# A hybrid decoder layer on one core: the bias table's DMAs on ScalarE's queue, other buffers for the gates, and an output projection that starts in two passes

## The chip, the core and the metric

The kernel runs on one core of a Trainium2 chip. The core has a matrix engine (TensorE, PE in the profile; its weight loads are PEld), VectorE (DVE), ScalarE (ACT), GpSimd (POOL) and SyncE (SP), which here issues DMAs. Each engine works through its own list of instructions in order, and semaphores hold an instruction until what it reads is there. The metric is the device time of one execution in microseconds.

## What is computed

One layer of a decoder, 512 tokens of width 1024, batch 1, float32:

```python
h = rms_norm(x, norm_mix)
qa, ka, va, qg, kg, vg, glr, rg = split(h @ w_in)
o_a = moba_attention(qa, ka, va, rp_table)           # 8 heads of 64, blocks of 256, relative bias
log_a = log_sigmoid(glr @ w_gate_up + b_gate) / 16
o_g = gla_chunked(qg, kg, vg, log_a)                  # 4 heads, decayed linear attention
o_g = rms_norm(o_g, g_norm) * silu(rg)
x = x + concat([o_a, o_g]) @ w_out
x = x + cross_attention(rms_norm(x, norm_xattn), rms_norm(mem, norm_mem))   # 256 memory tokens, 4 heads
x = x + square(relu(rms_norm(x, norm_mlp) @ w_up)) @ w_down
return rms_norm(x, norm_final)
```

With 512 tokens and blocks of 256 every past block is chosen, so the block-sparse group is plain causal attention with a bias by distance.

## The kernel before, in words

Activations lie transposed: 8 tiles of 128 rows (k-tiles) by 512 tokens. Each float32 operand is split into a high and a low float16 half, and a product is three float16 products (high by high, high by low, low by high: L231 to L233, for token-major results L246 to L248, in the later matrix products L1183 to L1185). A weight tile of 128x1024 float32 is loaded by SP into a buffer `wst` (5 of them, L114); ScalarE makes the high half `whl` (10 buffers, L115) and VectorE the low half (L116). `Weights.order` lists the tiles in the order in which they are loaded, and `get` asks for some tiles ahead.

TensorE's order is written by hand, that of the other engines is made by a scheduler from the program. Work that nobody waits for soon is a generator in a queue, `Fill`: `fill(n)` lets TensorE do n steps of it, and a step of a 128x512 product is one k-tile, three products. So the gated linear attention (class `Gla`, two passes for two pairs of heads) is laced with `vg` (values), `qk` (queries and keys of the attention), `xk` and `xv` (keys and values of the memory tokens) at L744 to L786. In `Gla`, a decay chain `e`, `g`, `b` gives scaled queries and keys (`qF`, `kF`, `qz`, `kz`, `z`), which TensorE multiplies into `psL`, `ps64`, later `st` and `go`; `gss` is the norm's sum. Then come the attention pairs 0 to 3 (class `Pair`, L787 and following): scores `s` at L809, `trans`, and `attn_out` one pair later, laced with `va`, `qk2`, `qk3` and the gates `rg`.

`rg_steps(h)` (L527) computes x times sigmoid of x by exponentials: after the product `rg` VectorE evicts it to `x`, ScalarE and VectorE work in turns in `e` and `u`, then the result multiplies `mixf[4 + h]` and is split into `mix[4 + h]`. The three float32 tiles came from one ring of 3 buffers (`yx`, shared with `qkf`, the eviction of `qk`). `early_steps` (L865) starts the output projection of row tiles 0 to 3 on the six k-tiles of `mix` that don't depend on the last two pairs (0, 1 from attention, 4 to 7 from the gates); `residual_steps` adds k-tiles 2 and 3 later.

The relative bias is made once: a small product (`bv`), a copy `bvec` by VectorE, a DMA to DRAM `bscr1` (L723) and a second DMA (L726) that spreads it over 128 rows, each shifted by one, into `bscr` (1.5 MB). `load_bias` reads from there (L739). The second DMA reads what the first wrote, so the queue that issues it waits for the first to land.

Of the kernel before, what the change touches and what calls it, by code (L numbers as in the profile page):

```python
# [10 lines left out]
F32 = mybir.dt.float32  # L11
# [5 lines left out]
P = 128  # L17
T = 512
# [21 lines left out]
def hybrid_block_kernel(  # L40
# [3 lines left out]
    nc = tc.nc  # L44
# [10 lines left out]
    pst = ctx.enter_context(tc.tile_pool(name="pst", bufs=2))  # L55
# [3 lines left out]
    def bank(tag, bufs, name):  # L59
        return psum.tile([P, 512], F32, tag=tag, bufs=bufs, name=name)  # L60

    def gbank(name):
        return bank("pg", 3, name)

    def sbank(name):
        return bank("ps", 5, name)
# [139 lines left out]
    W.add(("tt", 8), w_tt[8])  # L206
    for n in range(4):
        W.add(("va", n), w_vv[n])
    for n in (2, 6, 3, 7, 9, 10, 11):
        W.add(("tt", n), w_tt[n])  # L210
    for nm, ap in (("out", w_out), ("xq", w_xq), ("xo", w_xo)):
        for n in range(8):
# [12 lines left out]
    def gemm_steps(ps, key, act, c0=0, c1=T, kts=range(8), start=True, stop=True, base=0, look=LOOK, **kw):  # L225
        wt = W.get(key, look).rearrange("p s (k c) -> p s k c", k=8)
        kts = list(kts)
        for i, kt in enumerate(kts):
            a = act[base + kt]
            st, sp = start and i == 0, stop and i == len(kts) - 1  # L230
            PE.matmul(ps, wt[:, 0, kt, :], a[:, 0, c0:c1], start=st, stop=False, **kw)  # L231
            PE.matmul(ps, wt[:, 0, kt, :], a[:, 1, c0:c1], start=False, stop=False, **kw)  # L232
            PE.matmul(ps, wt[:, 1, kt, :], a[:, 0, c0:c1], start=False, stop=sp, **kw)  # L233
            yield
# [5 lines left out]
    def gemm_tok_steps(ps, keys, act, t0, look=LOOK):  # L240
        ws = [W.get(k, look).rearrange("p s (k c) -> p s k c", k=2) for k in keys]
        for kt in range(8):
            w = ws[kt // 2]
            a = act[kt]
            st, sp = kt == 0, kt == 7
            PE.matmul(ps, a[:, 0, t0:t0 + P], w[:, 0, kt % 2, :], start=st, stop=False)  # L246
            PE.matmul(ps, a[:, 0, t0:t0 + P], w[:, 1, kt % 2, :], start=False, stop=False)
            PE.matmul(ps, a[:, 1, t0:t0 + P], w[:, 0, kt % 2, :], start=False, stop=sp)  # L248
            yield
# [24 lines left out]
    fill = Fill()  # L274

    def split(dst_h, dst_l, src, scale):
        ACT.activation(dst_h, src, AF.Copy, scale=scale)  # L277
        DVE.scalar_tensor_tensor(dst_l, src, scale, dst_h, op0=ALU.mult, op1=ALU.subtract)  # L278
# [76 lines left out]
    mix = [m.bitcast(F16).rearrange("p (s t) -> p s t", s=2) for m in mixf]  # L355
# [15 lines left out]
    def tmp(nm):  # L371
        return p1.tile([P, T], F32, tag="yx", bufs=3, name=nm)
# [12 lines left out]
    for j in range(4):  # L385
        for i, _ in enumerate(W.pieces(2)):
# [5 lines left out]
            sq = acc if k % 4 == 0 else pst.tile([P, 512], F32, tag="sq", bufs=2, name=f"sqx{k}")  # L392
# [6 lines left out]
    for j in range(4):  # L399
        w = W.tiles["gqk", j][1].rearrange("p s (k n c) -> p s k n c", k=2, n=4)  # L400
        for i in range(2):
            x = act0[2 * j + i]
            for n, ps in enumerate(gps):
                for a, b in ((0, 0), (0, 1), (1, 0)):
                    PE.matmul(ps, w[:, a, i, n, :], x[:, b, :], start=(j == 0 and i == 0 and a == 0 and b == 0),
                              stop=(j == 3 and i == 1 and a == 1), skip_group_check=True)
# [7 lines left out]
    def evict(dst, ps, scale):  # L414
        DVE.scalar_tensor_tensor(dst, ps, scale * IX, wx, op0=ALU.mult, op1=ALU.mult)

    for n, ps in enumerate(gps):
        t = (gq, gk)[n % 2][n // 2] = pg.tile([P, T], F32, name=f"gqk{n}")
# [9 lines left out]
    for i in range(2):  # L428
        for a, b in ((0, 0), (0, 1), (1, 0)):
            for j in range(4):  # L430
                kt = 2 * j + i
                PE.matmul(psg[32 * j:32 * j + 32, :], wg[:, a, kt, :], act0[kt][:, b, :],
                          start=(i == 0 and a == 0 and b == 0), stop=(i == 1 and a == 1),
# [12 lines left out]
    def va_steps(t):  # L446
        ps = gbank(f"va{t}")
        yield from gemm_tok_steps(ps, [("va", j) for j in range(4)], act0, t * P)
        va[t] = p1.tile([P, 2, 512], F16, tag="va", bufs=4, name=f"vas{t}")
        split(va[t][:, 0, :], va[t][:, 1, :], ps, wxt[:, t:t + 1])  # L450
# [3 lines left out]
    def qk_steps(p):  # L454
        for lst, col, sc in ((aq, 0, 0.125), (ak, 4, 1.0)):
            ps = gbank(f"qk{col + p}")
            yield from gemm_steps(ps, ("tt", col + p), act0)
            nm = f"qks{col + p}"
            lst[p] = p1.tile([P, 2, T], F16, tag="qk", bufs=6, name=nm) if p < 3 else pt.tile([P, 2, T], F16, name=nm)
            y = tmp(f"qkf{col + p}")  # L460
            evict(y, ps, SA * sc)
            split(lst[p][:, 0, :], lst[p][:, 1, :], y, 1.0)
# [64 lines left out]
    def rg_steps(h):  # L527
        ps = gbank(f"rg{h}")
        yield from gemm_steps(ps, ("tt", 8 + h), act0)
        x, e, u = (tmp(f"rg{c}{h}") for c in "xeu")  # L530
        evict(x, ps, 1.0)
        ACT.activation(e, x, AF.Exp, scale=-1.0)
        DVE.tensor_scalar(e, e, 1e30, None, op0=ALU.min)
        ACT.activation(u, e, AF.Ln, bias=one_c)
        ACT.activation(u, u, AF.Exp, scale=-1.0)

        DVE.scalar_tensor_tensor(e, e, 1.0, u, op0=ALU.add, op1=ALU.mult)
        DVE.scalar_tensor_tensor(u, e, 2.0, u, op0=ALU.subtract, op1=ALU.mult)
        DVE.scalar_tensor_tensor(x, x, -1.0, u, op0=ALU.mult, op1=ALU.mult)
        DVE.tensor_tensor(x, x, mixf[4 + h], op=ALU.mult)  # L540
        split(mix[4 + h][:, 0, :], mix[4 + h][:, 1, :], x, 1.0)


    class Gla:
# [175 lines left out]
    bvec = pst.tile([P, 512], F32, tag="sq", bufs=2, name="bvec")[0:8, :NDIST]  # L720
    DVE.tensor_copy(bvec, psb[0:8, 0:NDIST])
    bscr1 = pdr.tile([8, NDIST], F32, name="bscr1")
    nc.sync.dma_start(bscr1, bvec)  # L723
    bscr = pdr.tile([8, P, T], F32, name="bscr")

    nc.sync.dma_start(  # L726
        bass.AP(tensor=bscr.tensor, offset=bscr.offset, ap=[[P * T, 8], [T + 1, P], [1, NDIST]]),
        bass.AP(tensor=bscr1.tensor, offset=bscr1.offset, ap=[[NDIST, 8], [0, P], [1, NDIST]]),
    )
# [4 lines left out]
    def load_bias(p):  # L734
        bias[p] = []
        for hh in range(2):
            h = 2 * p + hh
            bq = (pt if p % 2 else p1).tile([P, T], F32, tag="bq", bufs=2, name=f"bq{h}")
            nc.sync.dma_start(bq[:, 256:], bscr[h, :, 127:383])  # L739
            POOL.tensor_copy(bq[:, :256], bq[:, 256:257].to_broadcast([P, 256]))  # L740
            bias[p].append(bq)
# [3 lines left out]
    fill.add(*[xv_steps(c, t) for c in range(2) for t in range(2)])  # L745
    gl = []
    for pr in range(2):
        fill(5)
        gl.append(Gla(pr))
        if pr == 0:  # L750
            pw_ = sbank("wxt")
            for t in range(4):
                PE.transpose(pw_[:, t * P:t * P + P], wx[:, t * P:t * P + P], ident)
            DVE.tensor_scalar(wxt, pw_.rearrange("p (n t) -> p n t", t=P)[:, :, 0], SA * IX, None, op0=ALU.mult)
    for pr in range(2):
        if pr == 1:
            load_bias(0)
        G = gl[pr]
        a = G.prep_fine()
        fill(18 if pr == 0 else 6)  # L760
        G.banks()
        G.small(0, a)
        for i, s in enumerate((8, 16)):
            a = G.prep_level(s)
            fill(4)
            G.small(128 + 128 * i, a)
        a = G.prep_level(32)
        fill(6)
        G.mid(a[0])
        a = G.prep_level(64)  # L770
        fill(6)
        G.large(a[0])
        G.prep_cross()
        fill(6)
        G.keys()
        fill(6)
        G.states()
        fill(6)
        G.outp()
        fill(6)  # L780
        for hh in range(2):
            G.norm(hh)
            fill(4)
        if pr == 0:
            fill.add(rg_steps(0))
# [76 lines left out]
    NPRE = 4  # L862
    early = {}

    def early_steps():  # L865
        for n in range(NPRE):
            early[n] = sbank(f"out{n}")
            yield from gemm_steps(early[n], ("out", n), mix, 0, T, (0, 1, 4, 5, 6, 7), stop=False, skip_group_check=True)

    def residual_steps(nm, act, hf, ssq):  # L870
        c0 = hf * HT
# [17 lines left out]

    HT = T // 2  # L890
    ssq = sums("out", *HALVES)
    fill.add(*[va_steps(t) for t in range(4)], qk_steps(2), qk_steps(3), *[rg_steps(h) for h in (1, 2, 3)])
    pairs = {}
    for i in range(5):
        if i < 4:
            pairs[i] = Pair(i)
            if i < 3:
                load_bias(i + 1)
        if i in (2, 3):
            fill.until({2: 4, 3: 3}[i])  # L900
        if i == 4:
            fill.drain()
            load_xr()
            fill.add(early_steps(), residual_steps("out", mix, 0, ssq[0]))
        for g in range(4):
            if i < 4:
                pairs[i].score(3 - g)
                fill(5 if i < 3 else 3)
            elif g > 0:
                fill(4)  # L910
            if 1 <= i < 4 and g == 3:
                fill.until(5)
                attn_out(pairs.pop(i - 1))
        if i < 4:
            pairs[i].trans()
            fill(4)
# [333 lines left out]
    for j in range(2):  # L1250
        for m in range(4):
            u = Unit(m, j)
# [31 lines left out]
    u, v = Unit(2, 1), Unit(3, 1)  # L1284
# [127 lines left out]
```

## Time and profile before

| what | us |
|---|---|
| runs of the kernel before | 723.3, 726.82, 727.47; median 726.82 |
| the profiled execution | 728.34 |
| its span, from first to last record | 726.6 |
| TensorE busy | 685.3 (94%) |
| VectorE busy | 553.3 (76%) |
| ScalarE busy | 416.6 (57%) |
| GpSimd busy | 75.1 (10%) |
| mean granted clock of TensorE | 0.976 |

The granted clock is 1.00 when TensorE has its full 2.4 GHz and 0.50 at 1.2 GHz. The times of all rows are microseconds from the start of the span; a row's bracket says how long the engine was idle before it and what ended that.

### The profile page before, as it was taken

The numbers are of one execution on the slowest core, as the hardware profiler recorded it, in microseconds if no ns is written. First come the engines' busy times: TensorE is split into PE (matmuls) and PEld (weight loads), VectorE is DVE, ScalarE is ACT, GpSimd is POOL, SyncE is SP. The second block draws the span as 40 slices with busy tenths as digits, with TensorE's granted clock in tenths as the row PEclk, the third lists the DMA queues.
The fourth block names the chain that finished last, engine by engine and source line by source line (L and its number), as shares of the span: only waits on it lengthen the run. The fifth ranks groups of instructions, "written<-read, shape, count | busy, mean of one in ns | idle before, by whom it ended". The sixth has DMA issues, their size and how long they took to land.

```text
span 726.6 us, 13422 instructions
## 1 busy us (share of the span) xinstructions
PE 685.3 (94%) x5352; PEld 469.6 (65%) x5352; DVE 553.3 (76%) x987; ACT 416.6 (57%) x800; POOL 75.1 (10%) x90
## 2 busy tenths in 40 slices
PE   8998959999899499799999999999999999999995
PEld 3444637444444168588888864458888866478884
DVE  6978378868968615847647899989887889999725
ACT  7655366677757315546535676555444666665533
POOL 4050000000000024200013200000000000003211
PEclk9999979999999799999999999999999999999998
DMA  8871009742837503306411513113333342314003
GB/s 301 268 254 41 1 6 295 262 135 80 240 89 214 160 1 106 127 3 174 145 30 47 188 53 122 58 59 117 117 116 117 116 143 90 117 34 143 29 1 117
DMA packets 57059, 85.68 MB, mean 118 GB/s; under 512 B 32123, under 2 KB 37540, under 8 KB 56996
## 3 DMA queue, kind: packets, MB, share of 16 engines
q1 hardware_dynamic: 56996, 84.82, 37.3%
q8 instruction: 42, 0.69, 0.4%
q14 instruction: 21, 0.17, 0.1%
HBM read 75.36 MB, written 3.68 MB: 109 GB/s over the span
## 4 chain that ended last, share of the span: by engine, by line
PE 59%; DVE 8%; ACT 3%; issue 1%; POOL 1%; DVEq 0%; ACTq 0%; POOLq 0%
PE up L232 6%; PE up L231 6%; PE up L233 6%; PE a L1183 4%; PE a L1185 4%; PE a L1184 4%; PE xq L232 2%; PE xq L233 2%; PE xq L231 2%; PE c L1184 2%; PE c L1183 2%; PE c L1185 2%; DVE whl L116 2%; PE out L232 1%; PE out L233 1%
## 5 line engine op out<-in xcount | busy, mean ns | idle before, releaser
L116 DVE SCALAR_TENSOR_TENSOR whl<-wst,whl 128x1024 f16<-128x1024 f32 (+1 forms) x165 | 195.2, 1190 | 26.7 <-ACT whl L115 26.1
L115 ACT ACTIVATE whl<-wst 128x1024 f16<-128x1024 f32 (+1 forms) x165 | 165.4, 1013 | 38.4 <-PE a L1185 7.9
L231 PEld LDWEIGHTS <-whl 128*128 128x128 f16 x744 | 73.6, 99 | 48.0 <-ACT whl L115 7.9
L232 PEld LDWEIGHTS <-whl 128*128 128x128 f16 x744 | 73.6, 99 | 47.7 <-issue 13.5
L233 PEld LDWEIGHTS <-whl 128*128 128x128 f16 x744 | 73.6, 99 | 46.3 <-issue 6.9
L231 PE MATMUL up<-act,whl 128*128 128x512 f16 (+1 forms) x224 | 78.1, 349 | 0.0
L233 PE MATMUL up<-act,whl 128*128 128x512 f16 (+1 forms) x224 | 78.1, 349 | 0.0
L232 PE MATMUL up<-act,whl 128*128 128x512 f16 (+1 forms) x224 | 78.1, 349 | 0.0
L1183 PE MATMUL a<-t,whl 128*128 128x256 f16 x192 | 52.3, 273 | 1.1 <-ACT v L1200 1.1
L1184 PE MATMUL a<-t,whl 128*128 128x256 f16 x192 | 52.3, 273 | 0.0
L1185 PE MATMUL a<-t,whl 128*128 128x256 f16 x192 | 52.3, 273 | 0.0
L1184 PEld LDWEIGHTS <-whl 128*128 128x128 f16 x456 | 44.6, 98 | 6.9 <-issue 1.5
L1183 PEld LDWEIGHTS <-whl 128*128 128x128 f16 x456 | 44.6, 98 | 5.2
L1185 PEld LDWEIGHTS <-whl 128*128 128x128 f16 x456 | 44.6, 98 | 5.0
L231 PE MATMUL out<-mix,whl 128*128 128x256 f16 (+1 forms) x104 | 31.6, 304 | 8.3 <-ACT mix L277 8.3
L232 PE MATMUL xq<-act,whl 128*128 128x256 f16 x128 | 35.5, 277 | 3.3 <-DVE act L278 3.3
L231 PE MATMUL xq<-act,whl 128*128 128x256 f16 x128 | 35.5, 277 | 0.9 <-ACT act L277 0.9
L233 PE MATMUL xq<-act,whl 128*128 128x256 f16 x128 | 35.5, 277 | 0.0
L233 PE MATMUL xo<-ox,whl 128*128 128x256 f16 x128 | 34.9, 273 | 0.0
L231 PE MATMUL xo<-ox,whl 128*128 128x256 f16 x128 | 34.9, 273 | 0.0
L232 PE MATMUL xo<-ox,whl 128*128 128x256 f16 x128 | 34.9, 273 | 0.0
L277 ACT ACTIVATE t<-hs 128x512 f16<-128x512 f32 x32 | 19.8, 624 | 24.0 <-DVE hs L1065 23.8
(334 smaller groups left out, 1646.7 us busy)
## 6 DMA issues: line engine op xcount, KB each, us to landing
wst<-in_w_up SPq DMA_DIRECT2D x32, 512.0 KB, 3.5
wst<-in_w_down SPq DMA_DIRECT2D x32, 512.0 KB, 3.8
wst<-in_w_tt SPq DMA_DIRECT2D x12, 512.0 KB, 4.7
wst<-in_w_vv SPq DMA_DIRECT2D x8, 512.0 KB, 5.1
wst<-in_w_xk SPq DMA_DIRECT2D x8, 512.0 KB, 11.2
wst<-in_w_xv SPq DMA_DIRECT2D x8, 512.0 KB, 5.0
wst<-in_w_out SPq DMA_DIRECT2D x8, 512.0 KB, 3.8
wst<-in_w_xq SPq DMA_DIRECT2D x8, 512.0 KB, 3.5
```

What stands on the lines that cost most here:

```text
L115: ACT.activation(wt[:, 0, c], stg[:, c], AF.Copy, scale=SW)
L116: DVE.scalar_tensor_tensor(wt[:, 1, c], stg[:, c], SW, wt[:, 0, c], op0=ALU.mult, op1=ALU.subtract)
L231: PE.matmul(ps, wt[:, 0, kt, :], a[:, 0, c0:c1], start=st, stop=False, **kw)
L232: PE.matmul(ps, wt[:, 0, kt, :], a[:, 1, c0:c1], start=False, stop=False, **kw)
L233: PE.matmul(ps, wt[:, 1, kt, :], a[:, 0, c0:c1], start=False, stop=sp, **kw)
L277: ACT.activation(dst_h, src, AF.Copy, scale=scale)
L1183: PE.matmul(ps, w[:, 0, kt, :], b[:, 0, c], start=st, stop=False, skip_group_check=not start)
L1184: PE.matmul(ps, w[:, 0, kt, :], b[:, 1, c], start=False, stop=False, skip_group_check=not start)
L1185: PE.matmul(ps, w[:, 1, kt, :], b[:, 0, c], start=False, stop=sp, skip_group_check=not start)
```

## The change

Five edits; the functions' arithmetic is the same.

```diff
-    for n in (2, 6, 3, 7, 9, 10, 11):
+    for n in (2, 6, 9, 3, 7, 10, 11):
         W.add(("tt", n), w_tt[n])
...
         yield from gemm_steps(ps, ("tt", 8 + h), act0)
-        x, e, u = (tmp(f"rg{c}{h}") for c in "xeu")
+        x = tmp(f"rgx{h}")
+        e, u = (pst.tile([P, 512], F32, tag=t, bufs=2, name=f"rg{t}{h}") for t in ("sq", "nw"))
...
-    nc.sync.dma_start(bscr1, bvec)
+    nc.scalar.dma_start(bscr1, bvec)
...
-    nc.sync.dma_start(
+    nc.scalar.dma_start(
         bass.AP(tensor=bscr.tensor, offset=bscr.offset, ap=[[P * T, 8], [T + 1, P], [1, NDIST]]),
...
-        fill(5)
+        fill(8 if pr == 0 else 4)
         gl.append(Gla(pr))
...
-        fill(18 if pr == 0 else 6)
+        fill(20 if pr == 0 else 6)
...
-        for n in range(NPRE):
-            early[n] = sbank(f"out{n}")
-            yield from gemm_steps(early[n], ("out", n), mix, 0, T, (0, 1, 4, 5, 6, 7), stop=False, skip_group_check=True)
+        for kts in ((0, 1, 4, 5), (6, 7)):
+            for n in range(NPRE):
+                if n not in early:
+                    early[n] = sbank(f"out{n}")
+                yield from gemm_steps(early[n], ("out", n), mix, 0, T, kts, start=kts[0] == 0, stop=False, skip_group_check=True)
...
-    fill.add(*[va_steps(t) for t in range(4)], qk_steps(2), qk_steps(3), *[rg_steps(h) for h in (1, 2, 3)])
+    fill.add(*[va_steps(t) for t in range(4)], qk_steps(2), rg_steps(1), qk_steps(3), rg_steps(2), rg_steps(3))
...
-            fill.until({2: 4, 3: 3}[i])
+            fill.until({2: 4, 3: 2}[i])
```

From L527 on a line of the changed kernel has a number higher by 1, from `early_steps` on by 2 or 3. In the rows below a name ends in its tile's number and a running number of the allocation.

ScalarE, early: `whl13` is the last weight split before the memory tokens are split (`mix0` to `mix3`; `accm`, `sqm` are their squares), `e0` opens the decay chain of the first head pair, `vgs` evict `vg`. Before:

```order
L115 ACTIVATE whl13_444<-wst13_443 128x1024
L483 ACTIVATE mix0_105<-memf0_841,gmem_400 128x256 x2
L486 ACTIVATE accm_845<-memf0_841 128x512
L483 ACTIVATE mix1_106<-memf1_842,gmem_400 128x256 x2
L490 ACTIVATE sqm1_860<-memf1_842 128x512
L483 ACTIVATE mix2_107<-memf2_843,gmem_400 128x256 x2
L490 ACTIVATE sqm2_867<-memf2_843 128x512
L483 ACTIVATE mix3_108<-memf3_844,gmem_400 128x256 x2
L490 ACTIVATE sqm3_874<-memf3_844 128x512
L115 ACTIVATE whl14_879<-wst14_878 128x1024
L556 ACTIVATE e0_467<-z0_463,gsb_76 128x512
```

The same place in the changed kernel:

```order
L115 ACTIVATE whl13_444<-wst13_443 128x1024
L724 DMA bscr1_413<-bvec_411 8x384
L483 ACTIVATE mix0_105<-memf0_803,gmem_400 128x256 x2
L486 ACTIVATE accm_807<-memf0_803 128x512
L483 ACTIVATE mix1_106<-memf1_804,gmem_400 128x256
L727 DMA bscr_415<-bscr1_413 8x128x384
L557 ACTIVATE e0_476<-z0_472,gsb_76 128x512
L444 ACTIVATE vgs0_491<-vg0_417,wxt_125 128x512
L558 ACTIVATE e0_476<-e0_476 128x512
L444 ACTIVATE vgs1_539<-vg1_493,wxt_125 128x512
L559 ACTIVATE e0_476<-e0_476,ones_78 128x512
L444 ACTIVATE vgs2_566<-vg2_541,wxt_125 128x512
```

The two DMAs stand between the first steps on the memory tokens, `e0` and three `vgs` have moved ahead of the rest of these steps, and `whl14` has moved behind them.

ScalarE, the weight splits `whl16` to `whl20` (the tiles 3 to 7 of `xk`). Before, behind steps of the second head pair (`kF_1`, `qz8_1`, `qz16_1`):

```order
L577 ACTIVATE kF_1_1166<-dF_1_1163 128x512
L594 ACTIVATE qz8_1_1253<-d8_1_1251 128x32x8
L595 ACTIVATE kz8_1_1254<-d8_1_1251 128x32x8
L594 ACTIVATE qz16_1_1329<-d16_1_1327 128x16x16
L115 ACTIVATE whl16_976<-wst16_975 128x1024
L115 ACTIVATE whl17_981<-wst17_980 128x1024
L115 ACTIVATE whl18_986<-wst18_985 128x1024
L115 ACTIVATE whl19_991<-wst19_990 128x1024
L115 ACTIVATE whl20_1045<-wst20_1044 128x1024
```

In the changed kernel, among steps of the first head pair (`qz16_0`, `z32_0`, `z64_0`):

```order
L595 ACTIVATE qz16_0_686<-d16_0_684 128x16x16
L596 ACTIVATE kz16_0_687<-d16_0_684 128x16x16
L115 ACTIVATE whl14_841<-wst14_840 128x1024
L657 ACTIVATE et0_890<-b0_481 128x4
L115 ACTIVATE whl15_914<-wst15_913 128x1024
L115 ACTIVATE whl16_976<-wst16_975 128x1024
L595 ACTIVATE z32_0_740<-d32_0_738 128x8x32
L596 ACTIVATE z32_0_740<-d32_0_738 128x8x32
L595 ACTIVATE z64_0_787<-d64_0_785 128x4x64
L596 ACTIVATE z64_0_787<-d64_0_785 128x4x64
L115 ACTIVATE whl17_981<-wst17_980 128x1024
L115 ACTIVATE whl18_986<-wst18_985 128x1024
```

The splits of one head pair's time have moved into the other's.

VectorE, ahead of the scores of attention pair 3: `qkf7` and `qks7` evict and split its keys, `rgx1` is gate 1, `pq2` the split probabilities of pair 2, `mix1` the output of pair 1. Before:

```order
L415 SCALAR_TENSOR_TENSOR qkf7_2334<-qk7_2263,wx_124 128x512
L814 TENSOR_SCALAR sm4_2_2170<-sm4_2_2170 128x2
L116 SCALAR_TENSOR_TENSOR whl47_2752<-wst47_2751,whl47_2752 128x1024
L278 SCALAR_TENSOR_TENSOR qks7_2333<-qkf7_2334,qks7_2333 128x512
L820 RECIPROCAL sm4_2_2170<-sm4_2_2170 128x4
L821 TENSOR_SCALAR sm4_2_2170<-sm4_2_2170 128x4
L838 SCALAR_TENSOR_TENSOR pq2_0_2238<-p2_1_0_2286,sm4_2_2170,pq2_0_2238 128x2x128
L838 SCALAR_TENSOR_TENSOR pq2_1_2239<-p2_1_1_2288,sm4_2_2170,pq2_1_2239 128x2x128
L838 SCALAR_TENSOR_TENSOR pq2_0_2238<-p2_0_0_2316,sm4_2_2170,pq2_0_2238 128x128
L838 SCALAR_TENSOR_TENSOR pq2_1_2239<-p2_0_1_2318,sm4_2_2170,pq2_1_2239 128x128
L278 SCALAR_TENSOR_TENSOR mix1_106<-o1_2359,mix1_106 128x512
L415 SCALAR_TENSOR_TENSOR rgx1_2399<-rg1_2338,wx_124 128x512
```

In the changed kernel (the other steps of gate 1 stand ahead of these rows):

```order
L278 SCALAR_TENSOR_TENSOR mix5_110<-rgx1_2258,mix5_110 128x512
L822 TENSOR_SCALAR sm4_2_2170<-sm4_2_2170 128x4
L278 SCALAR_TENSOR_TENSOR qks3_2342<-qkf3_2343,qks3_2342 128x512
L278 SCALAR_TENSOR_TENSOR mix1_106<-o1_2368,mix1_106 128x512
L839 SCALAR_TENSOR_TENSOR pq2_0_2238<-p2_1_0_2295,sm4_2_2170,pq2_0_2238 128x2x128
L839 SCALAR_TENSOR_TENSOR pq2_1_2239<-p2_1_1_2297,sm4_2_2170,pq2_1_2239 128x2x128
L839 SCALAR_TENSOR_TENSOR pq2_0_2238<-p2_0_0_2325,sm4_2_2170,pq2_0_2238 128x128
L839 SCALAR_TENSOR_TENSOR pq2_1_2239<-p2_0_1_2327,sm4_2_2170,pq2_1_2239 128x128
L415 SCALAR_TENSOR_TENSOR qkf7_2409<-qk7_2347,wx_124 128x512
L116 SCALAR_TENSOR_TENSOR whl48_2815<-wst48_2814,whl48_2815 128x1024
L278 SCALAR_TENSOR_TENSOR qks7_2408<-qkf7_2409,qks7_2408 128x512
```

Gate 1, which began behind `mix1`, now ends ahead of `qks3`, and `qks7` has moved behind `mix1` and the `pq2`, to the end of the queue ahead of pair 3's scores.

## Rows read from the trace of the kernel before

**Rows 1.** TensorE's waits, whole span: line, waited for, total us, times, longest.

```profile
PE out L231 <- ACT mix L277: 8.3, 2, 5.4
PE xk L231 <- ACT whl L115: 7.6, 1, 7.6
...
PE psL L609 <- DVE kF L579: 1.6, 1, 1.6
...
PE z L552 <- DVE glr L415: 1.4, 1, 1.4
...
PE out L232 <- DVE mix L278: 0.8, 1, 0.8
...
PE xk L233 <- DVE whl L116: 0.7, 1, 0.7
```

**Rows 2.** Stretches: length, busy PE, PEld, DVE, ACT, POOL (count), PEclk, DMA, GB/s.

```profile
106.00:108.00 2.00, 1.27 (x6) 0.60 (x7) 2.00 (x3) 2.00 (x3) 0.00 (x0) 0.50 0.00 0
108.00:110.00 2.00, 2.00 (x11) 1.44 (x10) 2.00 (x3) 1.72 (x2) 0.00 (x0) 0.50 0.84 244
110.00:112.00 2.00, 2.00 (x12) 1.41 (x11) 0.68 (x1) 0.00 (x0) 0.00 (x0) 0.52 0.90 253
```

**Rows 3.** The same view after two later waits.

```profile
200.00:202.00 2.00, 2.00 (x9) 0.64 (x6) 1.36 (x5) 0.00 (x0) 0.00 (x0) 0.67 1.05 238
202.00:204.00 2.00, 2.00 (x6) 0.66 (x5) 0.12 (x1) 1.52 (x4) 0.00 (x0) 0.50 0.67 248
248.00:250.00 2.00, 1.46 (x4) 0.42 (x4) 0.69 (x1) 0.35 (x1) 0.00 (x0) 0.50 0.07 27
250.00:252.00 2.00, 2.00 (x7) 0.71 (x6) 0.00 (x0) 0.00 (x0) 0.00 (x0) 0.53 0.00 0
```

**Rows 4.** ScalarE in order of time: start, us, what, count, idle before.

```profile
34.92 1.06 ACT L115 ACTIVATE whl<-wst 128x1024 f16<-128x1024 f32 x1 [0.29 <-DMA wst<-in_w_xk]
...
44.22 0.63 ACT L490 ACTIVATE sqm<-memf 128x512 f32<-128x512 f32 x1 [3.32 <-POOL accm L491]
...
45.70 0.67 ACT L556 ACTIVATE e<-z,gsb 128x512 f32<-128x512 f32 x1
...
104.89 4.83 ACT L115 ACTIVATE whl<-wst 128x1024 f16<-128x1024 f32 x5
```

**Rows 5.** SP in order of time, the DMAs of the bias table.

```profile
34.34 0.30 SPq L723 DMA_DIRECT2D bscr<-bvec  x1
...
38.92 0.77 SPq L726 DMA_DIRECT2D bscr<-bscr  x1
```

**Rows 6.** DMA issues: count, KB each, median us to landing.

```profile
wst<-in_w_xk SPq DMA_DIRECT2D x8, 512.0 KB, 11.2
```

**Rows 7.** TensorE in order of time: products 1 and 54 of one stretch, then psL.

```profile
42.85 0.38 PE L246 MATMUL vg<-whl,act 128*128 128x512 f16 x1
...
54.29 0.38 PE L248 MATMUL vg<-whl,act 128*128 128x512 f16 x1
56.31 0.76 PE L609 MATMUL psL<-qF,kF 64*32 64x32 f32 x64 [1.64 <-DVE kF L579]
```

**Rows 8.** The costliest groups: VectorE's weight split, total, mean ns, idle before.

```profile
L116 DVE SCALAR_TENSOR_TENSOR whl<-wst,whl 128x1024 f16<-128x1024 f32 (+1 forms) x165 | 195.2, 1190 | 26.7 <-ACT whl L115 26.1
```

**Rows 9.** VectorE in order of time: the eviction of gate 1.

```profile
220.69 0.69 DVE L415 SCALAR_TENSOR_TENSOR rgx<-rg,wx 128x512 f32<-128x512 f32 x1 [0.26 <-PE rg L233]
```

**Rows 10.** TensorE in order of time: the first scores of pairs 2 and 3.

```profile
198.54 0.39 PE L809 MATMUL s<-qks,qks 64*128 64x512 f16 x2 [1.02 <-ACT qks L277]
...
221.23 0.82 PE L809 MATMUL s<-qks,qks 64*128 64x512 f16 x6
```

**Rows 11.** Stretches of 10 us in the gated attention, columns as in rows 2.

```profile
50.00:60.00 10.00, 8.36 (x134) 3.98 (x133) 9.93 (x16) 5.88 (x11) 0.00 (x0) 1.00 0.34 128
70.00:80.00 10.00, 10.00 (x63) 4.86 (x61) 3.48 (x9) 3.16 (x9) 0.00 (x0) 1.00 0.00 0
```

## The prediction

> **What bounds the kernel now.** I read first the waits of TensorE, because TensorE is busy in 94% of the span. [Rows 1] holds the six waits that matter here, and they lie in two places. At 98 to 107 us TensorE stands still for the weight tiles of `xk` (7.6 us for ScalarE's high half at L115, 0.7 us for VectorE's low half at L116). At 238 to 248 us it stands still in the output projection for `mix` tiles (8.3 and 0.8 us). The two smaller ones (1.4 us for `glr`, 1.6 us for `kF`) open the gated attention.
>
> Then I read the stretches after the two big waits. [Rows 2]: from 106 to 112 us the granted clock is 0.50 to 0.52, so TensorE is at 1.2 GHz although it works. Of these 6 us it is busy 1.27 + 2.00 + 2.00 = 5.3 us; at 2.4 GHz that work takes half, so the wait costs another 2.6 us. [Rows 3]: after the second wait 1.46 us of 248 to 250 and, at 0.53, some 1.9 us of 250 to 252 run at 1.2 GHz, another 1.7 us. The waits are worth 7.6 + 0.7 + 1.4 + 1.6 + 2.6 = 13.9 us in the first part and 8.3 + 0.8 + 1.7 = 10.8 us in the second.
>
> Last I read why `xk` weights are late. It is no transfer: ScalarE does five splits (L115) in a row from 104.89 [rows 4], and in its order these five stand behind `qz16` of the second head pair, which waits for the whole chain of the first. ScalarE works in order, so the tiles lie loaded in their buffers.
>
> **The change: the first part.** The two DMAs of the bias table leave SP and stand on ScalarE's queue, the second behind a wait for the first to land. No DMA is added. The order rows above show what goes with it: `whl16` to `whl20`, the `xk` weights TensorE waited for, now stand before `z32` of the first pair, some 40 us earlier in the same work. Nothing that they wait for is late there: their slots are last read by the `vg` and `tt` products, which are done before `xk` starts. I take the 7.6, the 0.7 and the 2.6 us as gone.
>
> What the wait on ScalarE costs: on SP the first DMA was issued at 34.34 us and the second could go at 38.92 [rows 5], so 4.6 us to land; issue took 0.30 and 0.77 us. On ScalarE the first goes out behind the split that ends at 36.0 [rows 4], three short steps follow (2 us), then it waits until 36.0 + 4.6 = 40.6 and issues until 41.4. Behind it stand `e0`, the start of the decay chain, and the evictions of `vg0` to `vg2`. Before, `e0` ran at 45.70, behind a square that waited 3.3 us for GpSimd [rows 4]; now it runs at 41.4. So the stall of 2.5 us lies in a place where ScalarE then waits for TensorE's `vg1` anyway. No row shows a DMA issued by ScalarE. Bounds: if the wait costs nothing, the chain below is unchanged, because it hangs on `vg2`; if landing takes the 11.2 us of the slowest loads [rows 6], `e0` runs at 48 and the chain is late by about 1 us. I take 0, the value of the nearest row.
>
> The Trainium skill (DMA: Bandwidth & Descriptors, section Issuing engines are not separate DMA queues) says that issuing from another engine saves only the issuing sequencer's time, which would be 0.30 + 0.77 us here. The traces so far have nothing against it as a rule on transfers; it says nothing on the order of the splits. By it the sum would be that of the third rival.
>
> The fills: 8, 4 and 20 steps instead of 5, 5 and 18. A step is three 128x512 products, (54.29 - 42.85) / 53 = 0.216 us each [rows 7], so 0.65 us. The first `z` now stands behind three more steps, 1.9 us, which is more than its wait of 1.4; that wait goes. The first `psL` product comes four steps later: 56.31 - 1.64 - 1.40 + 4 x 0.65 = 55.9 us [rows 7]. Is `kF` there? ScalarE now does `vgs2` behind the end of `vg2`, which is 8 steps earlier at 50.7, then seven `mix` and square steps, `qF` and `kF`: 0.6 + 3.6 + 1.0 = 5.2 us (0.4 for a half-width and 0.5 to 0.6 for a full one, as the spacing of such steps in [rows 4]); VectorE's product adds 0.7. That is 56.7: a new wait of about 0.9 us in place of the 1.6.
>
> For the second pair `kF_1` is on the path, which the `xk` wait used to hide. After the last `gss` 10 short steps follow, 60 products of half the width at half of 0.216 us, 6.5 us. In this time ScalarE has eight steps (4.7 us, one split among them), and VectorE behind them a split of 1.19 us [rows 8] and four of 0.6: 7.6 us. New wait 1.1. For the splits that stand before `qks1` and `qz16` I add 0.5 and 0.2. New waits 0.9 + 1.1 + 0.7 = 2.7 us, all short. First part: 13.9 - 2.7 = 11.2 us gained.
>
> **The change: the second part.** The gate of head 1 goes ahead of `qk3`, the gates' `e` and `u` get buffers of their own, and out 0 to 3 go over k-tiles 0, 1, 4, 5 first and over 6, 7 afterwards. The second pass starts 48 products (4 x 12) later than the first, 10.4 us; before, the first tile wanted `mix6` after 12 products, 2.6 us. By that alone 7.8 us of the wait for `mix6` and `mix7` is covered, and gate 1's six VectorE steps no longer stand in the queue between gates 2 and 3.
>
> But these steps now stand in front of `qks7` in VectorE's row order, and `qk7` ends one step before the third pair's scores want it. At 220.69 VectorE had just waited 0.26 us for TensorE [rows 9], so it carried no backlog. Gate 1 adds 0.6 + 0.33 + 4 x 0.6 + 0.6 = 3.9 us (0.69 is one step's length, 0.6 its share of the queue) and a split 1.1 us. Against that stands about 1.3 us of idle time that it can use. So `qks7` is done near 220.4 + 3.9 + 1.1 - 1.3 + 0.7 = 224.8 and the scores at L809, which TensorE reached at 221.23 [rows 10], wait about 3.6 us. The same structure stands there already for the pair before, at 198.54 [rows 10], and after that wait the clock was 0.67 and 0.50 for 2 us each [rows 3]: 3.3 us at 1.2 GHz, a loss of 1.7. I take both: 5.3 us. Bounds: 0, if the backlog is hidden in idle time, and 10.8 us, if all of it comes back. Behind, gate 3 ends near 250 us and TensorE wants it near 250.6, so I count nothing. Second part: 10.8 - 5.3 = 5.5 us.
>
> **Sum.** 11.2 + 5.5 = 16.7 us. The profiled execution took 728.34 us (span 726.6), 1.5 above the median of 726.82 us. 728.34 - 16.7 = 711.6, and against the median 710.1 us. Behind 262 us every engine's order is that of before, so nothing should come back there.
>
> **The rivals.**
> 1. The gates only move the wait: `qks7` is so late that the second part gains nothing. For it: VectorE is the busy engine there. Against: the pass over 0, 1, 4, 5 gives TensorE 10.4 us of work. 728.34 - 11.2 - 1.5 = 715.6 us. The same time comes out if the `kF_1` chain costs 5.5 us more.
> 2. The new waits don't show: VectorE uses its idle time. 24.7 - 1.5 for the remainder gives a gain of 23.2: 703.6 us. For it: between 70 and 80 us VectorE is busy 3.48 of 10 us [rows 11].
> 3. The move of the two DMAs saves SP's issue time of 1.07 us alone and the `xk` wait stays. Then the fills' 3.0 us, the 1.07 and the 5.5 remain, 9.6 us: 717.2 us. Against it: the splits' place in the order.
> 4. It doesn't do what it says in sum: 10 us or more come back in the later stages, which wait for VectorE too. 720 to 733 us. Against it: the equal orders.
> 5. Slower: the 12 splits that now stand among the first pair's chain push that chain back, and TensorE, which has some 20 products in the gated attention that wait for it, waits at each. One split in front of each is 20 x 1.19 [rows 8] = 23.8 us, more than the 16.7: 733.9 us. It decides from 16.7 / 20 = 0.84 us at each. For it: VectorE is busy 9.93 of 10 us from 50 to 60 [rows 11]. Against: 3.48 from 70 to 80, and 4 to 6 steps (2.6 to 3.9 us) between the places.
>
> **How the numbers follow.** Forecast 0.52 (706 to 714), rival 1 0.19, rival 2 0.12, rival 3 0.05, rival 4 0.07, rival 5 0.05. The range leaves out rivals 4 and 5 and little else: 703.5 to 718. About 1% is what a measurement of this kernel can tell from no change; faster by more is 0.52 + 0.19 + 0.12 + 0.05 = 0.88, within it 0.07, slower 0.05.
>
> **What would show it.** Right: no wait of `xk` for L115 and a clock of 1.00 from 90 to 115; ScalarE's splits of `xk` before 75; `s` at L809 waiting twice for `qks`, the second time 2 to 5 us; no `out` wait over 1 us. Wrong: a wait over 3 us in the gated attention, a clock of 0.50 there, ScalarE's second DMA issued later than 46 us, or an `out` wait of several us that remains.

## The result, and the profile after

| | us |
|---|---|
| the kernel before, median of the runs beside it | 727.08 |
| the changed kernel, median of 4 runs | 715.31 (714.64 to 716.58) |
| ratio | 0.9852, 95% interval 0.9821 to 0.9883 |
| its profiled execution, and the span of it | 715.83, 714.0 |

By the medians the change gives 11.8 us; the ratio, 1.5%, puts it at 10.8 (8.5 to 13.0). The sums below go by medians. The kernel before had medians of 726.4 to 727.8 us beside the experiments, so a difference between two of them is good to about 1 to 2 us. Three executions, two of experiment 5 and one of experiment 8, took 1435 to 2501 us at a granted clock of 1.00 and are left out of the medians. The forecast was 710.1 us, so it was 5.2 us too hopeful, inside its range of 703.5 to 718. The mean granted clock rose from 0.976 to 0.983, and TensorE is busy for 682.5 us.

TensorE's waits in the changed kernel (line, waited for, total us, times, longest):

```profile
PE psL L610 <- DVE kF L580: 8.2, 2, 6.8
PE s L810 <- ACT qks L277: 4.4, 2, 2.7
...
PE s L810 <- DVE qks L278: 1.1, 2, 0.7
```

Against [rows 1], the waits of `xk`, of `out` and of `z` are gone. In their place stands one that the prediction had at 0.9 us: the first `psL` product waits 6.8 us for `kF`. TensorE in order of time (start, us, what, idle before and its releaser):

```profile
61.56 0.89 PE L610 MATMUL psL<-qF,kF 64*32 64x32 f32 x64 [6.79 <-DVE kF L580]
...
111.55 0.75 PE L610 MATMUL psL<-qF,kF 64*32 64x32 f32 x64 [1.38 <-DVE kF L580]
...
192.28 0.39 PE L810 MATMUL s<-qks,qks 64*128 64x512 f16 x2 [1.69 <-ACT qks L277]
193.35 0.61 PE L810 MATMUL s<-qks,qks 64*128 64x512 f16 x4 [0.68 <-DVE qks L278]
...
215.75 0.61 PE L810 MATMUL s<-qks,qks 64*128 64x512 f16 x2 [2.67 <-ACT qks L277]
216.83 1.03 PE L810 MATMUL s<-qks,qks 64*128 64x512 f16 x4 [0.47 <-DVE qks L278]
```

Stretches of the changed kernel (length; busy time of PE, PEld, DVE, ACT, POOL with counts; granted clock; DMA share; GB/s):

```profile
56.00:60.00 4.00, 0.00 (x0) 0.00 (x0) 0.87 (x2) 2.05 (x4) 3.80 (x5) 0.83 0.00 0
60.00:64.00 4.00, 2.44 (x68) 1.35 (x69) 4.00 (x7) 3.98 (x9) 2.02 (x5) 0.50 0.00 0
64.00:68.00 4.00, 4.00 (x77) 1.93 (x76) 4.00 (x7) 2.93 (x7) 0.00 (x0) 0.82 0.02 4
...
192.00:196.00 4.00, 3.04 (x16) 1.20 (x16) 2.78 (x7) 0.60 (x2) 0.00 (x0) 1.00 1.12 255
196.00:200.00 4.00, 4.00 (x24) 1.60 (x22) 1.88 (x6) 1.93 (x7) 0.00 (x0) 1.00 0.52 163
...
216.00:220.00 4.00, 3.54 (x12) 0.96 (x10) 2.25 (x7) 0.48 (x1) 0.00 (x0) 0.50 1.14 258
220.00:224.00 4.00, 4.00 (x18) 1.27 (x17) 1.20 (x5) 1.04 (x4) 0.00 (x0) 0.69 0.53 163
```

TensorE runs at 1.2 GHz behind the `psL` wait. 2.44 us of work at 0.50 lose 1.2 us, and at 0.82 some 1.4 of the 4 us are at half clock and lose 0.7: 1.9 us. Behind pair 3's scores it loses 1.8 + 1.2 = 3.0 us in the same way. Behind pair 2's scores, where [rows 3] had 0.67 and 0.50, the clock now stays at 1.00 in this execution.

ScalarE's splits of the `xk` tiles 2 to 7 in the changed kernel:

```profile
64.21 1.99 ACT L115 ACTIVATE whl<-wst 128x1024 f16<-128x1024 f32 x2
...
68.56 1.99 ACT L115 ACTIVATE whl<-wst 128x1024 f16<-128x1024 f32 x2
...
75.59 1.06 ACT L115 ACTIVATE whl<-wst 128x1024 f16<-128x1024 f32 x1 [1.34 <-DMA wst<-in_w_xk]
...
78.00 1.06 ACT L115 ACTIVATE whl<-wst 128x1024 f16<-128x1024 f32 x1 [1.35 <-DMA wst<-in_w_xk]
```

Five of them ran from 104.89 us before [rows 4]; now all are done by 79.1, and the first `xk` product runs at 89.6. The prediction's sign, before 75, missed the last two, which waited 1.3 us each for their tiles; that cost TensorE nothing.

Why `kF` is late is read backwards from it, engine by engine. VectorE, ScalarE and GpSimd of the changed kernel around 50 to 61 us:

```profile
59.13 0.69 DVE L579 TENSOR_TENSOR qF<-qF,gqk 128x512 f32<-128x512 f32 x1 [4.53 <-ACT qF L577]
59.74 1.76 DVE L580 TENSOR_TENSOR kF<-kF,gqk 128x512 f32<-128x512 f32 x1
```

```profile
51.92 0.62 ACT L490 ACTIVATE sqm<-memf 128x512 f32<-128x512 f32 x1
...
57.95 0.63 ACT L490 ACTIVATE sqm<-memf 128x512 f32<-128x512 f32 x1 [4.61 <-POOL accm L491]
58.49 0.61 ACT L577 ACTIVATE qF<-dF 128x512 f32<-128x512 f32 x1
59.01 0.61 ACT L578 ACTIVATE kF<-dF 128x512 f32<-128x512 f32 x1
```

```profile
55.85 0.84 POOL L741 COPY bq<-bq 128x256 f32<-128x256 f32 x2 [15.78 <-DMA bq<-bscr]
56.66 4.30 POOL L491 TENSOR_TENSOR accm<-accm,sqm 128x512 f32<-128x512 f32 x3
```

`kF` stands on ScalarE behind the third square `sqm`. That square reuses the buffer of the first, which GpSimd has to add to `accm` first. In GpSimd's row the copies of `bq0` and `bq1` now stand ahead of the additions, and they wait for SP's read of the bias table. So a queue whose order the prediction had not read had changed. A second cost is in VectorE's row: the product for `kF` takes 1.76 us where `qF`, just before it, takes 0.69.

The two transfers themselves, SP and ScalarE's queue, did what was forecast:

```profile
53.65 0.81 SPq L740 DMA_DIRECT2D bq<-bscr  x2
```

```profile
34.03 0.55 ACTq L724 DMA_DIRECT2D bscr<-bvec  x1
...
38.99 0.73 ACTq L727 DMA_DIRECT2D bscr<-bscr  x1
39.77 0.69 ACT L557 ACTIVATE e<-z,gsb 128x512 f32<-128x512 f32 x1 [2.99 <-DVE wxt L755]
...
44.44 0.69 ACT L444 ACTIVATE vgs<-vg,wxt 128x512 f32<-128x512 f32 x1 [2.90 <-PE vg L248]
```

The second goes out 5.0 us behind the first, `e0` runs at 39.8 instead of 45.7 [rows 4], and ScalarE then waits 2.9 us for TensorE: the stall is covered. The read of the table goes out only at 53.65.

### The profile page after: what moved, and what is told of

It reads as the page before. It is cut to its first block, busy times and chain, and to the rows that moved or that the text cites. A ratio compares the mean times of both kernels' runs of the same rounds, so it can differ in the third digit from the quotient of the medians.

```text
span 714.0 us, 13411 instructions
## 1 busy us (share of the span) xinstructions
PE 682.5 (96%) x5352; PEld 469.4 (66%) x5352; DVE 551.7 (77%) x987; ACT 417.0 (58%) x800; POOL 73.6 (10%) x90
## 4 chain that ended last, share of the span: by engine, by line
PE 56%; DVE 7%; ACT 3%; issue 2%; POOL 1%; DVEq 0%; ACTq 0%; POOLq 0%
PE up L233 6%; PE up L231 6%; PE up L232 6%; PE a L1186 4%; PE a L1187 4%; PE a L1188 4%; PE xq L232 2%; PE xq L233 2%; PE xq L231 2%; PE c L1187 2%; PE c L1186 2%; PE c L1188 2%; DVE whl L116 1%; PE xo L233 1%; PE xo L232 1%
## 5 line engine op out<-in xcount | busy, mean ns | idle before, releaser
L231 PEld LDWEIGHTS <-whl 128*128 128x128 f16 x744 | 73.4, 99 | 39.8 <-issue 4.5
L232 PEld LDWEIGHTS <-whl 128*128 128x128 f16 x744 | 73.4, 99 | 38.4 <-issue 3.8
L232 PE MATMUL up<-act,whl 128*128 128x512 f16 (+1 forms) x224 | 78.1, 349 | 0.0
L232 PE MATMUL xq<-act,whl 128*128 128x256 f16 x128 | 36.0, 281 | 3.3 <-DVE act L278 3.3
L232 PE MATMUL xo<-ox,whl 128*128 128x256 f16 x128 | 34.9, 273 | 0.0
L232 PE MATMUL out<-mix,whl 128*128 128x256 f16 (+1 forms) x104 | 30.9, 297 | 0.1
```

## The experiments

Twelve kernels, each against the kernel before on the same chip. Theory A is the reading above.

**1. The additions on VectorE.** The changed kernel with

```diff
-                POOL.tensor_tensor(accm, accm, sq, op=ALU.add)
+                DVE.tensor_tensor(accm, accm, sq, op=ALU.add)
```

> The changed kernel with one engine altered: the three additions of squares to accm in mem_steps run on VectorE and no longer on GpSimd, so that GpSimd's copies of bq0 and bq1 stand ahead of nothing that the fine gates wait for. Theory A (the 6.8 us at the first psL product come from GpSimd's queue: the bq copies wait there for the bias table, the additions stand behind them, ScalarE's third square waits for an addition and qF and kF stand behind that square): the wait falls to under 2 us, the granted clock of 56 to 64 us is above 0.9, and the median is 706 to 710 us (715.3 less 6.8 less the 1.9 of the clock, up to 3 given back). Theory B (ScalarE's own queue, held by the two bias transfers and the weight splits, makes kF late): the wait stays above 4 us and the median is 713 to 716. Theory C (the wait goes, but the chain after it is set by the loads of the memory's weights): under 2 us at psL, a new wait of some 5 us or more at the xk products, median 712 to 716.

Measured: 709.82 us, ratio 0.9753 (0.9728 to 0.9778). TensorE, ScalarE and GpSimd in order of time:

```profile
56.30 0.76 PE L610 MATMUL psL<-qF,kF 64*32 64x32 f32 x64 [1.30 <-DVE kF L580]
```

```profile
53.49 0.61 ACT L490 ACTIVATE sqm<-memf 128x512 f32<-128x512 f32 x1
54.01 0.61 ACT L577 ACTIVATE qF<-dF 128x512 f32<-128x512 f32 x1
```

```profile
56.37 2.82 POOL L741 COPY bq<-bq 128x256 f32<-128x256 f32 x2 [18.53 <-DMA bq<-bscr]
```

GpSimd waits for the table even longer (18.53 us against 15.78 in the changed kernel), but nobody waits for GpSimd: `qF` leaves ScalarE 4.5 us earlier, `psL` waits 1.3 us, and the clock from 52 to 68 us is 1.00. Wait and clock cost 7.4 us less; the medians differ by 5.5 and the ratios by 7.2, so A fits within what the runs can tell. B and C fall.

**2. GpSimd's order alone.** The additions stay on GpSimd, and the first two copies are made to wait for them:

```diff
-            POOL.tensor_copy(bq[:, :256], bq[:, 256:257].to_broadcast([P, 256]))
+            wide = bq[:, 256:257].to_broadcast([P, 256])
+            if p:
+                POOL.tensor_copy(bq[:, :256], wide)
+            else:
+                POOL.tensor_scalar(bq[:, :256], mem_acc[0][:, :256], 0.0, None, op0=ALU.mult)
+                POOL.tensor_tensor(bq[:, :256], bq[:, :256], wide, op=ALU.add)
```

> The changed kernel with the order of GpSimd alone altered: the additions stay on GpSimd at their 1.43 us each, and the copies of bq0 and bq1 are made to depend on accm (each becomes a product of accm with zero and an addition of the wide column), so that they stand behind the additions. Theory A (it is the copies' wait for the bias table in front of the additions, 15.8 us of idle time in GpSimd's queue): psL waits under 2 us, the clock of 56 to 64 us stays at 1.00, and the median is 707.5 to 711 us, as with the additions on VectorE. Theory K (it is the additions' length on GpSimd, 4.3 us for three against 0.7 each on VectorE): psL waits 4 us or more, median 713 to 716.

Measured: 712.9 us, ratio 0.9795 (0.9755 to 0.9835), `psL` waits 4.41 us. Neither number fits A: the wait is the one K gave, and the median lies between the two. GpSimd's queue does what A says (the additions begin at 51.33, and the third square waits for nothing), but now VectorE is late. GpSimd and VectorE in order of time:

```profile
51.33 5.14 POOL L491 TENSOR_TENSOR accm<-accm,sqm 128x512 f32<-128x512 f32 x3 [13.91 <-ACT sqm L490]
```

```profile
52.23 1.43 DVE L484 SCALAR_TENSOR_TENSOR mix<-memf,gmem,mix 128x256 f16<-128x256 f32 x1
53.58 1.75 DVE L569 TENSOR_TENSOR dF<-g 128x512 f32<-128x512 f32 x1
55.26 1.75 DVE L569 TENSOR_TENSOR d<-b 128x512 f32<-128x512 f32 x1
...
57.60 0.67 DVE L579 TENSOR_TENSOR qF<-qF,gqk 128x512 f32<-128x512 f32 x1
```

While GpSimd adds, until 56.5, three of VectorE's operations take 1.43, 1.75 and 1.75 us; behind the additions `qF`, as wide as `dF`, takes 0.67. So the additions do matter, as K has it, but not by their length in GpSimd's queue: ScalarE, which waited for them, has `kF`'s exponential at 55.9 with no wait for GpSimd in front. This gave theory N.

**3. GpSimd busy, but waited for by nobody.** To part the queue from the company it keeps: the additions to `accm` on VectorE, GpSimd adding the squares into an unread tile, the copies as in 2.

```diff
-                POOL.tensor_tensor(accm, accm, sq, op=ALU.add)
+                DVE.tensor_tensor(accm, accm, sq, op=ALU.add)
+                POOL.tensor_tensor(junk, sq, sq, op=ALU.add)
```

> The run copies_behind_adds with the additions to accm on VectorE, while GpSimd adds each square to itself into a tile that nothing reads, at the place where the additions stood; nothing of the output waits for GpSimd there. Theory N (in copies_behind_adds the rest of the wait came from GpSimd's additions running beside VectorE's: dF, d and one half of mix took 1.75, 1.75 and 1.43 us there against 0.68, 0.68 and 0.46 beside an idle GpSimd): one or two of VectorE's operations with two operands in SBUF between 52 and 58 us take 1.4 to 1.8 us again though no semaphore ties them to GpSimd, psL waits 3 to 5 us, median 711.5 to 714.5. Theory O (what counts is only who waits for GpSimd's queue): these operations stay at 0.5 to 0.7 us, psL waits under 2 us, median 708 to 711.

Measured: 712.72 us, ratio 0.9783 (0.9749 to 0.9818); `psL` waits 3.78 us. Theory N holds. VectorE, and GpSimd beside it:

```profile
52.81 1.47 DVE L492 TENSOR_TENSOR accm<-accm,sqm 128x512 f32<-128x512 f32 x1
54.20 1.52 DVE L571 TENSOR_TENSOR dF<-g 128x512 f32<-128x512 f32 x1
55.64 1.52 DVE L571 TENSOR_TENSOR d<-b 128x512 f32<-128x512 f32 x1
```

```profile
51.84 3.33 POOL L493 TENSOR_TENSOR junk<-sqm 128x512 f32<-128x512 f32 x2 [11.32 <-ACT sqm L491]
55.47 1.15 POOL L493 TENSOR_TENSOR junk<-sqm 128x512 f32<-128x512 f32 x1 [0.30 <-ACT sqm L491]
```

No semaphore ties `dF` and `d` to GpSimd here, and they are stretched all the same. So the 6.8 us of the changed kernel are made of 4.5 us of GpSimd's queue (`qF` on ScalarE at 58.49 against 54.01 in experiment 1), 1.1 us of an addition beside `kF` (1.76 against 0.68) and the 1.3 that are left in experiment 1: 6.9 us.

**4. The transfers back on SP**, all else as changed:

```diff
-    nc.scalar.dma_start(bscr1, bvec)
+    nc.sync.dma_start(bscr1, bvec)
...
-    nc.scalar.dma_start(
+    nc.sync.dma_start(
```

> The changed kernel with only the first edit undone: both bias transfers back on SyncE's queue, all else as changed. Theory A: GpSimd's additions run before its bq copies again, psL waits under 1.5 us, and in its place the xk products wait again, 7 to 11 us, with the half clock behind them; median 718 to 724. Theory B (which queue issues the bias transfers does not matter, the gain of the first part is from the larger fill counts): no xk wait above 3 us, median 705 to 712. Theory D (the move is worth nothing and the wait only changed place): median 713 to 717.

Measured: 721.41 us, ratio 0.9893 (0.9851 to 0.9935). TensorE's waits:

```profile
PE psL L610 <- DVE kF L580: 3.6, 2, 3.3
...
PE xk L231 <- ACT whl L115: 2.7, 1, 2.7
PE xk L233 <- DVE whl L116: 1.9, 1, 1.9
```

The time is A's, and so is the exchange (the first `psL` waits 0.4, `xk` waits again); but `xk` waits 4.6 us where A said 7 to 11, and 3.3 us are `kF` of the second pair, which A had not named. ScalarE begins four `xk` splits only at 96.7 us again, and GpSimd's additions stand ahead of its copies again. B and D fall.

**5. The transfers on ScalarE alone**, in the kernel before (the four lines of 4 in the other direction).

> The kernel before with only the first edit made: both bias transfers on ScalarE's queue, old fill counts, old gates, one pass. Theory A: GpSimd's copies stand ahead of its additions here too, psL waits 7 to 9 us, the xk wait of 11.2 us is gone, the wait at the output projection stays; the first part gives 4 to 7 us of the 11.8 that the whole change gave: median 720 to 723. Theory D (the move is worth nothing without the fill counts): 726 to 728. Theory E (the first part gives all of the gain): 714 to 717.

Measured: 724.09 us, the median of seven runs, ratio 0.9965 (0.994 to 0.999), which is 2.3 us less than before (726.4): between A and D, in the range of neither. The wait that comes is nearly as long as the one that goes. TensorE's waits:

```profile
PE psL L609 <- DVE kF L579: 8.4, 2, 7.2
PE out L231 <- ACT mix L277: 8.3, 2, 5.4
```

No `xk` wait is left, 8.3 us and the 2.6 of its clock, and ScalarE begins these splits at 62.9 us; `psL` waits 6.8 us more than in [rows 1], at half clock behind it. A had priced the larger fill counts into this run, which doesn't have them.

**6. The first part alone**: 5 with the fill counts of the change; gates, buffers and the one pass as before.

> The kernel before with the first part of the change alone: the bias transfers on ScalarE's queue and the larger fill counts; old gates, old order, one pass. Theory A: the xk wait of 11.2 us is gone, psL waits 6.8 us, the first part gives 5 to 6.5 us and the clock that stays up behind pair 2's first scores another 1 to 2: median 719 to 722. Theory E (the first part gives all of the gain): 714 to 717. Theory D (it gives nothing): 726 to 728.

Measured: 722.15 us, ratio 0.9925 (0.9901 to 0.9949), 0.15 above A's range. The first part gives 5.2 us (727.34 beside it), not 11.2. Waits: `psL` 6.0, `out` 8.3 as before.

**7. The gate order undone** in the changed kernel:

```diff
-    for n in (2, 6, 9, 3, 7, 10, 11):
+    for n in (2, 6, 3, 7, 9, 10, 11):
...
-    fill.add(*[va_steps(t) for t in range(4)], qk_steps(2), rg_steps(1), qk_steps(3), rg_steps(2), rg_steps(3))
+    fill.add(*[va_steps(t) for t in range(4)], qk_steps(2), qk_steps(3), *[rg_steps(h) for h in (1, 2, 3)])
...
-            fill.until({2: 4, 3: 2}[i])
+            fill.until({2: 4, 3: 3}[i])
```

> The changed kernel with the order of the gates undone: all of pair 3's queries and keys ahead of the gates 1 to 3, the weights loaded in the old order, and the count at pair 3 back at 3; the gates' buffers and the two passes stay. Theory A (the order, not the buffers or the passes, makes pair 3's first scores wait 2.7 + 0.5 us at half clock, some 5 to 6 us in all, and takes the wait ahead of the output projection away): the score waits fall under 1.5 us, but the second pass of the projection waits for mix7, 3 to 9 us; median 715 to 721. Theory F (the buffers alone take the projection's wait away, and the order only costs): the scores' and the projection's waits are both under 2 us and the median is 709 to 712.

Measured: 712.42 us, ratio 0.9789 (0.977 to 0.9808): 2.9 us less than the changed kernel by the medians, 4.6 by the ratios. TensorE's waits:

```profile
PE out L231 <- ACT mix L277: 2.0, 1, 2.0
PE s L810 <- ACT qks L277: 1.6, 1, 1.6
```

Pair 3's scores no longer wait (the 1.6 us are pair 2's), and the projection waits 2.0 us, not the 3 to 9 of A. On this point A was wrong, and the time is nearer to F's 709 to 712: by the rows the new order costs 3.1 us of waiting and 3.0 of clock to save 2.3 (2.0, and 0.3 for `mix` at L232).

**8. Old order, one pass** (7, and the loop over `kts` in `early_steps` undone: one pass over k-tiles 0, 1, 4, 5, 6, 7).

> The changed kernel with the gates in the old order and the first part of the output projection in one pass, as before; of the second part's edits only the gates' buffers stay. Theory J (the two passes carry the second part: the first pass's 48 products of 0.22 us, 10.4 us, hide the last gate, where one pass has 15 to 18 products, 3.2 to 3.9 us, before it needs mix7): the projection waits 7 to 9 us more in front of mix7 and runs at half clock behind it, median 719 to 723. Theory F (the gates' buffers carry it): the projection's wait stays under 3 us, median 712 to 714.

**9. Old order, old buffers** (7, and `x, e, u` from one ring again, two passes kept).

> The changed kernel with the gates in the old order and in their old buffers; of the second part's edits only the two passes stay. Theory J (the buffers are worth nothing here, since the last two gates take 11.5 and 7.8 us from rgx to the split of mix in the old buffers and in the new ones): median 711.4 to 713.4, as with the old order alone. Theory F: the gates 1 to 3 start later or take longer, the projection waits 4 us or more, median 716 to 721.

Measured: 722.88 us, the median of three runs (ratio 0.9931, 0.9909 to 0.9954), with one pass and 711.76 us (0.979, 0.9773 to 0.9806) with the old buffers; the first line is the projection's wait with one pass, the second with the old buffers:

```profile
PE out L231 <- ACT mix L277: 8.3, 2, 5.4
```

```profile
PE out L231 <- ACT mix L277: 2.0, 1, 2.0
```

Theory J holds. Of the second part the two passes carry everything: 722.15 (run 6) less 711.76 is 10.4 us. The buffers carry nothing that can be told from noise (711.76 without them, 712.42 with them), so F falls as well.

**10. The best of both**: 1 and 7 together.

> The changed kernel with two things altered: the three additions to accm on VectorE, and the gates in the order of the kernel before. Theory A (the two costs lie in different stages and add up): psL waits under 2 us, pair 3's first scores under 1.5 us, the projection under 3 us; median 706.9 us (709.8 of the run with the additions alone less the 2.9 that the old order alone gave), 705 to 708.5. Theory H (one is given back where the other goes, later in the program): 709 to 711.

Measured: 706.89 us (706.08 to 707.31), ratio 0.9718 (0.9704 to 0.9733), what A had added up; that it fits to the decimal is luck. It beats the changed kernel by 8.4 us. Its waits:

```profile
PE psL L610 <- DVE kF L580: 2.7, 2, 1.4
PE out L231 <- ACT mix L277: 2.0, 1, 2.0
```

**11. The same with the old fill counts** (5 and 18 for 8 and 20, 5 for 4).

> The run adds_dve_old_order with the fill counts of the kernel before (5 and 18 in place of 8 and 20, 5 in place of 4). Theory A (the larger counts give TensorE work until kF is there, some 4 us of it, since the wait at psL was 7.2 us with the old counts and the additions in the way, and 6.0 to 6.9 with the new): psL waits 2 to 5 us, at half clock behind it, median 709 to 714. Theory L (with the additions out of the way kF is early enough for either count): psL waits under 2 us, median 706 to 708.5.

Measured: 712.91 us, ratio 0.9793 (0.976 to 0.9826). TensorE:

```profile
58.81 0.89 PE L610 MATMUL psL<-qF,kF 64*32 64x32 f32 x64 [3.88 <-DVE kF L580]
```

The counts are worth 6.0 us once GpSimd is out of the way. A holds, L falls.

**12. The second part alone** (4 and the old fill counts).

> The kernel before with the second part of the change alone: new gate order, new buffers, two passes; bias transfers on SyncE's queue, old fill counts. Theory A (the parts add up; the second gives 10.4 us by the passes and loses 2.9 by the order): the xk wait of 11.2 us stands as before, the projection's wait is gone, pair 3's scores wait 2.7 us; median 718.5 to 721. Theory M (the clock and the weight splits tie the two parts together): outside 717 to 722.5.

Measured: 721.31 us, ratio 0.9911 (0.9882 to 0.9941), 0.3 above A's range and inside M's bounds, so M falls: `xk` waits 7.6 us for ScalarE as before, pair 3's scores 2.7, and the projection's wait is gone. It gives 6.1 us; with the 5.2 of run 6 that is 11.3 of the 11.8 us. The fill counts are in run 4 and not here, and both end at 721 us: the larger counts gain nothing while the transfers stand on SP.

## Why the prediction was right or wrong

The sign, the range and most of the mechanism were right; one step of the first part failed and two sizes of the second were off.

- **The `xk` wait and its clock, 10.9 us: right.** No `xk` wait is left, and the clock is 1.00 from 72 to 114 us. Both come back when the transfers go back to SP (4.6 us of waiting in run 4, 8.3 in run 12). The third rival, SP's issue time alone, would have ended near the measured time with the `xk` wait still there; it isn't. The Trainium skill's rule on issuing engines (DMA: Bandwidth & Descriptors, section Issuing engines are not separate DMA queues) speaks of transfers, and no row contradicts it there; by it alone, as an estimate from [rows 5], run 5 would gain 1.1 us, with the `xk` wait unchanged. Run 5 gains 2.3 and has no `xk` wait, because what moved is the order of other work.
- **The stall on ScalarE taken at 0: right**, with 5.0 us to land for the estimated 4.6.
- **"Is `kF` there? ... a new wait of about 0.9 us": the step that failed.** It counted ScalarE's seven `mix` and square steps as 3.6 us in a row. The last of these squares waits for GpSimd, whose row the change had turned round, and the 4.6 us of that wait were not in the sum. Nor was VectorE's 1.76 us. Measured: 6.8 us and 1.9 of clock. With GpSimd out of the way (run 1) the wait is 1.3, and the whole is 709.8 us against the 710.1 forecast. By the prediction's own list, a wait of over 3 us in the gated attention at 0.50 was to prove it wrong, and that is what the trace has. The sum itself reads 56.7 where its terms give 56.6, which does not matter here.
- **The other new waits, 1.1 + 0.7: 1.4 us at the second `kF`, none for `qks1` and `qz16`.** For the second `kF` the terms of the sum (4.7 + 1.19 + 4 x 0.6) give 8.3 us and not 7.6, so a wait of 1.8 and not 1.1; the measured one lies between. The clock behind pair 2's scores, 1.7 us lost before, was counted as unchanged and is now a gain; that the change caused it is not shown (see the last section). So the first part is 11.2 - 7.8 (8.7 for 0.9) + 0.4 + 1.7 = 5.5, against 5.2 in run 6.
- **The second part, 10.8 - 5.3 = 5.5 us: mechanism right, two terms off.** Pair 3's scores wait 3.1 for the predicted 3.6 and lose 3.0 for 1.7 at half clock, 6.1 us. But the order does not have to be paid for: the two passes alone give 10.4 us and leave a wait of 2.3, so the order costs 2.9 net and the part gives 10.4 - 2.9 = 7.5. Measured directly it is 6.8 (run 6 less the changed kernel) or 6.1 (run 12), so 5.5 was low by about 1 us. This miss went the other way than that of the first part (6.0 us too high) and hid a little of it. That the buffers or the gate's place would help was an assumption, and runs 7 and 9 show neither does.
- **Rival 1's time came out (715.6), its cause did not**: the wait it had at the second pair's `kF` lies at the first, and the gates' part gained. Rival 5, waits throughout the gated attention, did not come: TensorE is busy without a gap from 64 to 84 us. **"Nothing should come back behind 262 us": nearly.** The last `xq` wait ends 13.6 us earlier than before and the span is 12.6 shorter, so 1.0 us came back.

## What to carry to other kernels

When an instruction moves to another queue, print the new order of every engine, the idle ones too: an engine that is 10% busy and works in order can stop two others when a copy that waits for a transfer slips in front of an addition they need. Take a bundle apart before believing in its parts: here three edits made the gain (the transfers, the fill counts, the two passes), one (the buffers) was nothing and one (the gate order) cost 2.9 us or more. And where an engine's work is moved to make room, look at what runs beside it, not only at who waits for it.

## What was not expected of the hardware

VectorE's operations with two operands in SBUF take about 0.8 to 1.1 us longer while GpSimd adds: 1.75 and 1.52 us for `dF` and `d` against 0.68, 1.76 for `kF` against 0.68, 1.43 for half a `mix` against 0.46, on three kernels, once with no dependence between the engines. GpSimd pays too: its two copies took 0.84 us beside an idle VectorE and 2.82 beside a busy one. The Trainium skill (SBUF — State Buffer, section Who interferes with whom) says that these two engines share a pair of ports as an exclusive lock, that issue order decides who blocks, and that whoever issues first keeps the pair for the whole instruction. The rows agree in that the extra time stays below one addition of GpSimd (1.27 us beside an idle VectorE). In the changed kernel `qF` began at 59.13 and kept its 0.69 us, the third addition began behind it at 59.34 and took 1.61, and `kF` began inside that addition, at 59.74, and ended 0.55 us behind it. That it is a lock and not a split these rows do not prove.

The half clock did not follow every wait: behind pair 2's scores 1.02 + 0.95 us of waiting went with 0.67 and 0.50 in the kernel before, and 1.69 + 0.68 us with 1.00 in the changed one. The length of the wait does not set them apart: in experiment 12 the same 1.02 + 0.95 us went with 1.00, and in experiment 1 1.61 + 0.68 us went with 0.84 and 0.74 over 4 us each. It also varies between executions of one kernel: the four of experiment 1 had mean granted clocks of 0.981 to 0.990 and times of 711.26 to 707.99 us. What sets it apart was not tried, so a clock term read from one trace, such as the 1.7 us behind pair 2's scores, may be the execution's and not the change's.
